# A hybrid decoder layer: TensorE's work of the retention block in program order, products of ones while it waits for loads, and first factors summed by TensorE alone

## The chip, the cores and the metric

The kernel runs on one core of one Trainium2 chip. The core has a tensor engine (TensorE; PE in the profile, with its weight loads listed apart as PEld), a vector engine (VectorE, DVE), a scalar engine (ScalarE, ACT), a general engine (GpSimd, POOL) and a queue that issues transfers (SyncE, SP); ACT can issue transfers too. Each engine works through its own instructions in order and waits for others by semaphores. The metric is the device time of one execution in microseconds (us), smaller is better.

## The reference, cut to what matters

One decoder layer on x of 1024 positions by 1024 channels, in float32. The change lies in its first third: the modulation of x by c, and the retention heads.

```python
mod = silu(c) @ w_ada + b_ada                 # six vectors of 1024
sh1, sc1, g1, sh2, sc2, g2 = split(mod)
h = x * (1.0 + sc1) + sh1
proj = h @ w_in                               # q, k, v, forget gates; rq, rk, rv, rg
fox = forgetting_attention(fq, fk, fv, log_sigmoid(ff + b_f))     # 8 heads of 64
ret = retention(rq, rk, rv, rg)                                   # 4 heads of 128
...
def retention(q, k, v, g):                    # q and k are rotated by position first
    ...
    def step(R, xs):                          # over 8 chunks of 128 positions
        s = einsum('bhnd,bhmd->bhnm', qi, ki) * inner
        o = einsum('bhnm,bhmv->bhnv', s, vi) + einsum('bhnd,bhdv->bhnv', qi, R) * xi
        R = R * g_chunk + einsum('bhmd,bhmv->bhdv', ki * zeta, vi)
        return R, o
    ...
    return silu(g) * normalised(o)
...
x = layer_norm(ALPHA * x + g1 * (concat(fox, ret) @ w_out))
h = x * (1.0 + sc2) + sh2                     # then the MLP with a convolution, and a second norm
```

## The kernel before, in words

Every large product is made from three: the operands are split into a high part (fp32r) and the low rest, and TensorE adds high x high, high x low and low x high in PSUM (`three`). A wide product is 128 x 128 weights against 512 columns.

**First stage.** The contraction over the 1024 channels of h is cut into eight slices j of 128. For slice j the SP queue loads the weights of the modulation (`ada`, two tiles of 4 x 256), a slice of the first retention head's weights (`wrr`) and a slice of x transposed (`xt`), three slices ahead (`h_load`). The shift and the scale of the slice, called first factors here, are `m = sum over k of ada_k * cs_k`: DVE adds up most of the eight terms into `acc` (`h_acc`), and `h_mod` lets PE multiply the rest (`DIRECT`: two terms for the first three slices, one otherwise) and `acc` by one column each; these products have one column and write a few columns of the PSUM tile `m1`. ACT adds the bias (`mod`), makes `hhi` (the high part of the modulated x) and the modulated `xt`, and DVE makes `hlo = xt - hhi`. Then PE adds the slice to seven PSUM tiles (`fa`, `fb`: the chunks of 128 positions of head 0) by 21 wide products: seven with hhi and the weights' high part, seven with their low part (among which the next slice's `h_mod` is placed), seven with hlo.

**Retention.** What remains of the projection of the four heads goes chunk by chunk (`ret_proj`, 24 wide products into a PSUM tile `rp`, in two halves of 12). `ret_evac` copies a chunk to SBUF and rotates it (POOL and DVE). The recurrence of a chunk takes three groups of small products, in three half-steps that follow one another: `ret_a` transposes q and k (`pq`, copied to `qkT` by ACT), `ret_b` makes the scores and the chunk's part of the state (`pS`; DVE weights the scores to `sT` and updates `R`), `ret_c` makes the output (`po`). `emit(t)` writes the groups that belong to half-step t between two halves of the projection. When a head's chunks are done, DVE and POOL normalise and gate it (`ret_norm`, `ret_gate`) and PE transposes it (`ret_out`, `py`). Beside that, DVE adds up the other four modulation vectors from `ada2` (`mod_piece`, `macc`), which PE closes with one-column products `mc` or two row products `mr` (`mod_end`). Last comes the projection of v and of the forget gates (`v_proj`, `vp`).

**What sets the order.** All of this stands in one block that a planner orders: it simulates the engines in time and picks for each engine what it believes to be ready, so the order of the code counts only where the code says so. `queued(key, ...)` says so: each call stands behind the last one of the same key on its engine. Before the change it is used for the loads, the ACT and DVE work and the first factors of the first stage; the wide products and all of the retention are left to the planner. The rest of the kernel (attention, output projection, MLP) follows after about 300 us.

The line numbers in the profile are those of the kernel below. What goes through `queued` is listed under L230 (the first call of a key under L232), since that is where the instruction is made; `three` is L207 to L209.

Of the kernel before, what the change touches and what calls it, by code (L numbers as in the profile page):

```python
# [15 lines left out]
P = 128  # L16
# [15 lines left out]
def kernel(  # L32
# [69 lines left out]
    cs = cp.tile([P, ND], F32, tag="cs", name="cs")  # L102
    nc.sync.dma_start(cs, cT)
# [6 lines left out]
    nc.vector.tensor_tensor(out=cs, in0=cs, in1=cse, op=ALU.mult)  # L110
    for i in (0, 2):
        nc.vector.tensor_scalar(
            out=bcol[:, i, :], in0=bcol[:, i, :], scalar1=1.0, scalar2=None, op0=ALU.add
        )
    mod2 = cp.tile([P, 2, ND], F32, tag="mod2", name="mod2")
# [29 lines left out]
    def bcast_rows(src, n):  # L145
        return bass.AP(tensor=src.tensor, offset=src.offset, ap=[[0, P], [1, n]])


    gates = dp.tile([2, D], F32, tag="gates", name="gates")
# [16 lines left out]
    def mod_end(m, acc):  # L166
        if m < 2:
            pt = bank(f"mc{m}")
            for j in range(ND):
                nc.tensor.matmul(  # L170
                    pt[:, j:j + 1], acc[:, j * P:(j + 1) * P], ones[:, 0:1],
                    start=True, stop=True,
                )
            nc.vector.tensor_tensor(
                out=mod2[:, m, :], in0=pt[:, :ND], in1=bcol[:, 2 + m, :], op=ALU.add
            )
            return
        row = slot("R", [1, D], F32, f"grow{m}")
        nc.sync.dma_start(row, b_rows[m - 2:m - 1, :])
        for n in range(2):  # L180
            sl = slice(n * 512, (n + 1) * 512)
            pt = bank(f"mr{m}_{n}")
            nc.tensor.matmul(pt[0:1, :], ones[:, 0:1], acc[:, sl], start=True, stop=True)
# [8 lines left out]
    def ret_w(h, j, raw):  # L192
        tag = "X" if h % 2 == 0 else "VM"
        w = slot(tag, [P, 2, 512], F32R, f"wr{h}_{j}")
        nc.scalar.copy(w[:, 0, :], raw)
# [9 lines left out]

    def three(pt, ahi, alo, whi, wlo, start, stop):
        nc.tensor.matmul(pt, ahi, whi, start=start, stop=False)  # L207
        nc.tensor.matmul(pt, ahi, wlo, start=False, stop=False)  # L208
        nc.tensor.matmul(pt, alo, whi, start=False, stop=stop)  # L209

# [9 lines left out]

    DIRECT = {0: 2, 1: 2, 2: 2}

    hs = {}
    order = {}

    def queued(key, fn, *args, **kw):

        if key in order:
            with tc.issue_after(order[key].ins):
                order[key] = fn(*args, **kw)  # L230
        else:
            order[key] = fn(*args, **kw)  # L232

    def ret_consts():
# [11 lines left out]
        return tr, dec, rc, bfb, lnc, cw  # L246

    def h_load(j):
        if j >= ND:
            return  # L250
        a = [slot("VM", [P, 4, 256], F32, f"ada1_{j}_{k}") for k in range(2)]
        for k in range(2):
            queued("SP", nc.sync.dma_start, a[k], ada1[j, :, 4 * k:4 * k + 4, :])
        raw = slot("R", [P, 512], F32, f"wrr0_{j}")
        queued("SP", nc.sync.dma_start, raw, w_ret[0, :, j, :])
        xt = slot("VM" if j % 2 else "S", [P, S], F32, f"xt{j}")
        queued("SP", nc.sync.dma_start, xt, xT[j * P:(j + 1) * P, :])
        hs[j] = (a, raw, xt)
# [29 lines left out]
    def h_mod(j):  # L288
        a, _, xt, acc = hs[j]
        pt = m1[:, 2 * j:2 * j + 2]  # L290
        for i in range(2):
            sl = slice(i * P, (i + 1) * P)
            n = DIRECT.get(j, 1)
            for k in range(ND - n, ND):
                queued(
                    "PE", nc.tensor.matmul, pt[:, i:i + 1], a[k // 4][:, k % 4, sl],
                    cs[:, k:k + 1], start=(k == ND - n), stop=False,
                )
            queued("PE", nc.tensor.matmul, pt[:, i:i + 1], acc[:, sl], ones[:, 0:1],
                   start=(n == 0), stop=True)  # L300
        for i in range(2):
# [5 lines left out]
        sc, sh = mod1[:, j, 0:1], mod1[:, j, 1:2]  # L307
        queued("ACT", nc.scalar.activation, hi, xt, AF.Identity, scale=sc, bias=sh)
        queued("ACT", nc.scalar.activation, xt, xt, AF.Identity, scale=sc, bias=sh)
        hhi.append(hi)  # L310

    def h_lo(j):
# [3 lines left out]
        hlo.append(lo)  # L316


    for j in range(3):
        h_load(j)  # L320
    h_cast(0)
    h_acc(0)
    h_low(0)
    h_mod(0)
    w1 = []
    for j in range(ND):
        h_load(j + 3)
        if j + 1 < ND:
            h_cast(j + 1)
            h_acc(j + 1)  # L330
        h_lo(j)
        if j + 1 < ND:
            h_low(j + 1)
        if j + 3 == ND:
            tr, dec, rc, bfb, lnc, cw = ret_consts()
        if j + 1 == ND:
            with tc.issue_after(order["ACT"].ins):
                for q in range(0, ND, 2):
                    ret_load(1, q, w1)
            queued("SP", nc.sync.dma_start, cw, conv)  # L340
        hi, lo = hhi[j], hlo[j]
        for c in range(7):
            nc.tensor.matmul(first[c], hi[:, c * P:(c + 1) * P], w0[j][:, 0, :],
                             start=(j == 0), stop=False)
        for c in range(7):
            if c == 3 and j + 1 < ND:
                h_mod(j + 1)
            order["PE"] = nc.tensor.matmul(first[c], hi[:, c * P:(c + 1) * P], w0[j][:, 1, :],
                                           start=False, stop=False)
        for c in range(7):  # L350
            nc.tensor.matmul(first[c], lo[:, c * P:(c + 1) * P], w0[j][:, 0, :],
                             start=False, stop=(j == ND - 1))

# [3 lines left out]
    def ret_proj(h, c, ws, part, pt):  # L357
        if part == 0:
            pt = bank2(f"rp{h}_{c}")[:, :512]
        for j in range(4 * part, 4 * part + 4):  # L360
            three(pt, hhi[j][:, c * P:(c + 1) * P], hlo[j][:, c * P:(c + 1) * P],
                  ws[j][:, 0, :], ws[j][:, 1, :], j == 0, j == ND - 1)
        return pt
# [21 lines left out]
    def ret_a(h, c, st):  # L385
        row = st["st"][c // 2][:, c % 2, :]
        pq = bank(f"pq{h}_{c}")
        nc.tensor.transpose(pq[:, 0:128], row[:, 0:P], ident)
        nc.tensor.transpose(pq[:, 128:256], row[:, P:2 * P], ident)
        qkT = tmp([P, 256], F32, f"qkT{h}_{c}")  # L390
# [10 lines left out]
    def ret_b(h, c, st):  # L401
        row = st["st"][c // 2][:, c % 2, :]
        qkT, v = st["qkT", c], row[:, 2 * P:3 * P]
        pS = bank(f"pS{h}_{c}")
        nc.tensor.matmul(pS[:, 0:128], qkT[:, 128:256], qkT[:, 0:128], start=True, stop=True)
        if c < NT - 1:
            nc.tensor.matmul(pS[:, 128:256], st["kz"], v, start=True, stop=True)
        sT = sp.tile([P, P], F32, tag="sT", bufs=2, name=f"sT{h}_{c}")
# [13 lines left out]
    def ret_c(h, c, st):  # L422
        row = st["st"][c // 2][:, c % 2, :]
        q, v = row[:, 0:P], row[:, 2 * P:3 * P]
        po = bank(f"po{h}_{c}")
        nc.tensor.matmul(po[:, 0:128], st["sT"], v, start=True, stop=(c == 0))
        if c > 0:
            nc.tensor.matmul(
                po[:, 0:128], st["qkT", c][:, 0:128], st["R"][c - 1], start=False, stop=True
            )  # L430
# [40 lines left out]
    def ret_out(h, half, st):  # L471
        pt = bank(f"py{h}_{half}")
        for i in range(4):
            c = half * 4 + i
            nc.tensor.transpose(
                pt[:, i * P:(i + 1) * P], st["st"][c // 2][:, c % 2, 0:P], ident
# [123 lines left out]
    def v_proj(c, n):  # L600
        n0, n1 = (0, 256) if n == 0 else (256, 520)
        pt = bank2(f"vp{c}_{n}") if c % 2 else bank(f"vp{c}_{n}")
        for j in range(ND):
            three(pt[:, :n1 - n0], hhi[j][:, c * P:(c + 1) * P],
                  hlo[j][:, c * P:(c + 1) * P],
                  wv[j][:, 0, n0:n1], wv[j][:, 1, n0:n1], j == 0, j == ND - 1)
        if n == 1:
# [47 lines left out]
    def cum_forget(Lp):  # L655
        pc = bank("pcum")
        nc.tensor.matmul(pc[:, :64], tri, L.rearrange("p c h -> p (c h)"),
                         start=True, stop=False)
        nc.tensor.matmul(pc[:, :64], ones, Lp.rearrange("p c h -> p (c h)"),
                         start=False, stop=True)  # L660
# [5 lines left out]
    def cum_store(cum):  # L666
        pc = bank("pcumT")
        nc.tensor.transpose(pc[:64, :P], cum.rearrange("p c h -> p (c h)"), ident)
        cumT = tmp([64, P], F32, "cumT")
# [898 lines left out]
```

## Time and profile before

| | |
|---|---|
| median of 3 runs | 1253.63 us (1252.91 to 1255.43) |
| the profiled execution | 1255.27 us, span from first to last instruction 1253.5 us |
| TensorE busy | 1220.3 us, 97% of the span |
| VectorE, ScalarE, GpSimd busy | 929.4, 630.9 and 247.9 us |
| mean granted clock of TensorE | 0.994 |
| first wide product of the first stage | at 12.72 us |
| first product of the rest of the projection (`rp`) | at 64.33 us |
| projection of v and of the gates (`vp`) | from 243.9 us to about 300 us |

The times in the profile's rows are us from the start of the span. A row in order of time gives the start, the duration, engine and line, the operation with the tiles it writes and reads, how many such instructions are merged, and in brackets how long the engine sat idle before and what released it. Matmuls overlap one another, so that the pace is read from one start to the next. A float32 product of TensorE is listed as two instructions, an fp32r product and a transpose as one. The granted clock is given by the throttle's records; in the first 17 us of the span these read 1.00 while equal products take twice as long as later, so there the speed is read from the starts.

### The profile page before, as it was taken

The page shows a single profiled execution, that of the slowest core. Times are in us where ns is not written, and L with a number is a line of the kernel's source. Part 1 is how long each engine was busy: PE and PEld are TensorE (multiplying, and loading weights), DVE is VectorE, ACT ScalarE, POOL GpSimd, SP SyncE. Part 2 cuts the span into 40 slices and gives each one's busy share as a digit, 9 for nine tenths or more (in the row PEclk, how much of TensorE's full clock was granted, in tenths as well). Part 3 has the DMA queues.
Part 4 walks back from the last instruction along what each step waited for, and adds up shares of the span by engine and source line. Part 5 has one row for each costly group of instructions (what it writes and reads, how often), then busy time and mean ns, then how long its engine had stood idle before and what let it go on. Part 6 is the DMA issues. An engine that isn't in the chain of part 4 may idle for free.

```text
span 1253.5 us, 17244 instructions
## 1 busy us (share of the span) xinstructions
PE 1220.3 (97%) x6077; PEld 1017.6 (81%) x6077; DVE 929.4 (74%) x1774; ACT 630.9 (50%) x1144; POOL 247.9 (20%) x293
## 2 busy tenths in 40 slices
PE   6999999999999999899999999999999999999997
PEld 5788888898888887788788888888888878888886
DVE  6774685884787777846888778778778785876686
ACT  3633233333676667476865444545445464634352
POOL 0034252500333333500003221321100101000021
PEclk9999999999999999999999999999999999999999
DMA  9623143443134234323238877976544588965751
GB/s 353 214 89 135 59 134 124 151 137 120 52 118 143 91 104 151 135 76 109 85 114 208 190 187 197 215 184 165 148 137 127 143 245 265 346 218 185 269 185 67
DMA packets 86046, 199.79 MB, mean 159 GB/s; under 512 B 9860, under 2 KB 16196, under 8 KB 85960
## 3 DMA queue, kind: packets, MB, share of 16 engines
q1 hardware_dynamic: 73288, 175.62, 40.6%
q0 software_dynamic: 12672, 23.07, 11.6%
q8 instruction: 48, 0.79, 0.2%
q14 instruction: 38, 0.31, 0.1%
HBM read 165.06 MB, written 68.20 MB: 186 GB/s over the span
## 4 chain that ended last, share of the span: by engine, by line
PE 85%; DVE 7%; ACT 3%; DMA 3%; issue 1%; SPq 0%; POOL 0%; DVEq 0%; ACTq 0%; POOLq 0%
PE dX L1307 10%; PE dZ L1307 7%; PE uX L1123 6%; PE uX L1124 6%; PE uX L1125 6%; PE uY L1125 4%; PE uY L1124 4%; PE uY L1123 4%; PE rp L208 3%; PE rp L209 3%; PE rp L207 3%; PE pv L793 3%; DMA xt<-in_xT_dram 2%; PE qk L709 2%; PE qk L710 2%; PE qk L711 2%
## 5 line engine op out<-in xcount | busy, mean ns | idle before, releaser
L1296 DVE TENSOR_TENSOR dl<-dr,dh 128x1024 fp32r<-128x1024 f32 x66 | 80.1, 1238 | 36.6 <-ACT dh L1284 35.7
L1284 ACT CAST dh<-dr 128x1024 fp32r<-128x1024 f32 x66 | 67.9, 1050 | 75.0 <-DMA dr<-in_w_down_dram 35.4
L755 POOL TENSOR_TENSOR S<-S,dn 128x128 f32<-128x128 f32 (+3 forms) x64 | 74.0, 1161 | 150.6 <-DVE dn L754 97.7
L970 POOL DMA_DIRECT2D sd<-gd x22 | 18.1, 823 | 394.3 <-DMA sd<-y 230.3
L207 PE MATMUL rp<-wr,hhi 128*128 128x512 f32 x200 | 79.0, 395 | 1.3 <-ACT rst L367 1.3
L208 PE MATMUL rp<-wr,hhi 128*128 128x512 f32 x200 | 79.1, 396 | 0.5 <-POOL wr L197 0.5
L209 PE MATMUL rp<-wr,hlo 128*128 128x512 f32 x200 | 78.8, 394 | 0.0
L1307 PE MATMUL dX<-dl,dh 128*128 128x512 f32 x176 | 68.5, 389 | 0.0
L1307 PE MATMUL dX<-dh 128*128 128x512 f32 x176 | 68.5, 389 | 0.0
L1307 PE MATMUL dX<-dh,dl 128*128 128x512 f32 x176 | 68.5, 389 | 0.0
L1138 ACT COPY u<-uX 128x512 f32<-128x512 f32 x44 | 25.8, 586 | 72.7 <-PE uX L1125 72.7
L751 ACT ACTIVATE S<-S,mn 128x128 f32<-128x128 f32 (+3 forms) x64 | 49.9, 779 | 15.1 <-DVE mn L746 13.9
L709 PE MATMUL qk<-hhi,wqh 128*128 128x512 f32 x128 | 54.6, 426 | 0.0
L784 DVE TENSOR_TENSOR pt<-pt,pt 128x512 fp32r<-128x512 f32 (+2 forms) x96 | 50.8, 550 | 4.3 <-ACT pt L783 3.1
L746 DVE CUSTOM_DVE_ANT_0 S<-ps,nb 128x128 f32<-128x128 f32 (+3 forms) x64 | 48.0, 750 | 8.0 <-PE ps L744 5.6
L793 PE MATMUL pv<-pt,V 128*128 128x256 f32 x320 | 49.8, 293 | 2.4 <-DVE pt L784 1.2
L208 PE MATMUL op<-wol,mxs 128*128 128x512 f32 x128 | 50.4, 394 | 1.7 <-DVE wol L893 1.5
L711 PE MATMUL qk<-hhi,wql 128*128 128x512 f32 x128 | 51.6, 403 | 0.0
L207 PE MATMUL op<-woh,mxs 128*128 128x512 f32 x128 | 50.7, 398 | 0.9 <-DVE mn L746 0.9
L1307 PE MATMUL dZ<-dh 128*128 128x512 f32 x132 | 51.6, 391 | 0.0
L1307 PE MATMUL dZ<-dl,dh 128*128 128x512 f32 x132 | 51.4, 389 | 0.0
L1307 PE MATMUL dZ<-dh,dl 128*128 128x512 f32 x132 | 51.4, 389 | 0.0
(1057 smaller groups left out, 3830.6 us busy)
## 6 DMA issues: line engine op xcount, KB each, us to landing
ada<-in_ada_dram SPq DMA_DIRECT2D x48, 512.0 KB, 4.0
td<-in_w_down_dram SPq DMA_DIRECT2D x44, 256.0 KB, 5.5
wa<-in_w_up_dram SPq DMA_DIRECT2D x22, 512.0 KB, 5.0
wb<-in_w_up_dram SPq DMA_DIRECT2D x22, 512.0 KB, 4.0
gd<-y SPq DMA_DIRECT2D x22, 512.0 KB, 2.7
sd<-y SPq DMA_DIRECT2D x44, 256.0 KB, 3.6
dr<-sd SPq DMA_DIRECT2D x44, 256.0 KB, 4.4
dr<-td SPq DMA_DIRECT2D x44, 256.0 KB, 3.9
```

Of the source, the lines that this page charges most:

```text
L207: nc.tensor.matmul(pt, ahi, whi, start=start, stop=False)
L208: nc.tensor.matmul(pt, ahi, wlo, start=False, stop=False)
L209: nc.tensor.matmul(pt, alo, whi, start=False, stop=stop)
L709: nc.tensor.matmul(pt, whi[:, j, :], hhi[j][:, sl], start=(j == 0), stop=False)
L711: nc.tensor.matmul(pt, wlo[:, j, :], hhi[j][:, sl], start=False, stop=(j == ND - 1))
L755: nc.gpsimd.tensor_tensor(out=Ssb[:, :span], in0=Ssb[:, :span], in1=den.to_broadcast([P, span]), op=ALU.mult,)
L793: nc.tensor.matmul(pv[:, :256], V2[h][:, kb, :], pts[kb // 4][u][:, kb % 4, :], start=(kb == 0 and u == 0), stop=(kb == nkb - 1 and u == 1),)
L1123: nc.tensor.matmul(pt, whi, bh, start=start, stop=False, skip_group_check=True)
L1124: nc.tensor.matmul(pt, whi, bl, start=False, stop=False, skip_group_check=True)
L1125: nc.tensor.matmul(pt, wlo, bh, start=False, stop=stop, skip_group_check=True)
L1296: nc.vector.tensor_tensor(out=lo, in0=raw, in1=f(hi), op=ALU.subtract)
L1307: nc.tensor.matmul(pt, w_[:, 0, q], m_[:, 1, :], start=start and n_ == 0, stop=stop and n_ == 2, skip_group_check=True)
```

## The change

Six edits, all in the block of the first stage and the retention:

1. TensorE's work of the block goes through `queued("PE", ...)`, in the order in which the code is written: the wide products of the first stage, `ret_proj`, `v_proj`, the groups of small products, the transposes, `mc` and `mr`. In the first stage the code now writes the next slice's first factors as one piece ahead of the last ten wide products (ahead of the last six for slice 0). The first half-step of the recurrence is one later (`2 * NT - 1`).
2. `keep_on`: eleven products of `ones` with `ones` at the start and seven after the first factors of slice 0, into columns of `m1` that nothing reads.
3. The first factors of slice 0 are summed by TensorE alone (`DIRECT[0] = ND`): 16 one-column products, no `acc`.
4. `cs` and `bcol` are loaded through ACT's queue; the addition of 1 to `bcol` stands later on DVE. `xt` of slice 0 is loaded and turned to `hhi` in two halves.
5. From slice 3 on, the first of the terms of `acc` is made by ACT.
6. The casts of head 1's weights on ACT are set by `queued`: two of the eight ahead of slice 7's `mod`, the others behind its `xt`; the low parts follow on DVE.

```diff
     cs = cp.tile([P, ND], F32, tag="cs", name="cs")
-    nc.sync.dma_start(cs, cT)
+    nc.scalar.dma_start(cs, cT)
     bcol = cp.tile([P, 4, ND], F32, tag="bcol", name="bcol")
-    nc.sync.dma_start(bcol, b_cols)
+    nc.scalar.dma_start(bcol, b_cols)
...
@@ ret_w @@
+        if h == 1:
+            queued("ACT", nc.scalar.copy, w[:, 0, :], raw)
+            return w, raw
         nc.scalar.copy(w[:, 0, :], raw)
-        eng = nc.vector if h == 1 else nc.gpsimd
-        eng.tensor_tensor(out=w[:, 1, :], in0=raw, in1=f(w[:, 0, :]), op=ALU.subtract)
+        nc.gpsimd.tensor_tensor(out=w[:, 1, :], in0=raw, in1=f(w[:, 0, :]), op=ALU.subtract)
...
+    def in_turn(*args, **kw):
+        queued("PE", nc.tensor.matmul, *args, **kw)
+
+    def turn(*args):
+        queued("PE", nc.tensor.transpose, *args)
...
-    DIRECT = {0: 2, 1: 2, 2: 2}
+    DIRECT = {0: ND, 1: 2, 2: 2}
...
+    def h_cuts(j):
+        return [slice(0, 512), slice(512, S)] if j == 0 else [slice(0, S)]
...
@@ h_acc @@
-        acc = tmp([P, 256], F32, f"acc1_{j}")
-        for k in range(ND - DIRECT.get(j, 1)):
+        n = ND - DIRECT.get(j, 1)
+        acc = tmp([P, 256], F32, f"acc1_{j}") if n else None
+        for k in range(n):
             src = a[k // 4][:, k % 4, :]
-            if k == 0:
+            if k == 0 and j > 2:
+                queued("ACT", nc.scalar.activation, acc, src, AF.Copy, scale=cs[:, 0:1])
+            elif k == 0:
...
+    def keep_on(n):
+
+        for _ in range(n):
+            in_turn(m1[:, 256:384], ones, ones, start=True, stop=True)
...
     for j in range(3):
         h_load(j)
+    keep_on(11)
+    for i in (0, 2):
+        queued("DVE", nc.vector.tensor_scalar,
+               out=bcol[:, i, :], in0=bcol[:, i, :], scalar1=1.0, scalar2=None, op0=ALU.add)
     h_cast(0)
     h_acc(0)
     h_low(0)
     h_mod(0)
+    keep_on(7)
...
+        if j + 2 == ND:
+            ret_load(1, 0, w1)
         h_lo(j)
...
         if j + 1 == ND:
-            with tc.issue_after(order["ACT"].ins):
-                for q in range(0, ND, 2):
-                    ret_load(1, q, w1)
+            for q in range(2, ND, 2):
+                ret_load(1, q, w1)
             queued("SP", nc.sync.dma_start, cw, conv)
+            for w, raw in w1:
+                queued("DVE", nc.vector.tensor_tensor, out=w[:, 1, :], in0=raw,
+                       in1=f(w[:, 0, :]), op=ALU.subtract)
+            w1 = [w for w, _ in w1]
         hi, lo = hhi[j], hlo[j]
-        for c in range(7):
-            nc.tensor.matmul(first[c], hi[:, c * P:(c + 1) * P], w0[j][:, 0, :],
-                             start=(j == 0), stop=False)
-        for c in range(7):
-            if c == 3 and j + 1 < ND:
+        seq = [(c, t) for t in range(3) for c in range(7)]
+        for n, (c, t) in enumerate(seq):
+            if n == (15 if j == 0 else 11) and j + 1 < ND:
                 h_mod(j + 1)
-            order["PE"] = nc.tensor.matmul(first[c], hi[:, c * P:(c + 1) * P], w0[j][:, 1, :],
-                                           start=False, stop=False)
-        for c in range(7):
-            nc.tensor.matmul(first[c], lo[:, c * P:(c + 1) * P], w0[j][:, 0, :],
-                             start=False, stop=(j == ND - 1))
+            in_turn(first[c], (hi, hi, lo)[t][:, c * P:(c + 1) * P],
+                    w0[j][:, (0, 1, 0)[t], :],
+                    start=(j == 0 and t == 0), stop=(j == ND - 1 and t == 2))
...
-        nc.tensor.transpose(pq[:, 0:128], row[:, 0:P], ident)
-        nc.tensor.transpose(pq[:, 128:256], row[:, P:2 * P], ident)
+        turn(pq[:, 0:128], row[:, 0:P], ident)
+        turn(pq[:, 128:256], row[:, P:2 * P], ident)
...
-        ta = max(2 * n + A0, 2 * NT - 2 + n)
+        ta = max(2 * n + A0, 2 * NT - 1 + n)
```

The same replacement by `in_turn` or `turn` stands at `three` in `ret_proj` and `v_proj`, at `pS`, `po`, `py`, `mc`, `mr` and the two `pcum` products.

How this stands on PE, at three places. In these rows `m` is the PSUM tile of the first factors, `fa` one of the seven tiles of the first stage, `wr` a slice of weights, and the numbers count buffers.

PE at its start, up to the first wide product, before:

```order
L232 MATMUL m_107<-cs,ada_0_1_110 128x1
L230 MATMUL m_107<-cs,ada_0_1_110 128x1
L230 MATMUL m_107<-ones,acc_0_135 128x1
L230 MATMUL m_107<-cs,ada_0_1_110 128x1 x2
L230 MATMUL m_107<-ones,acc_0_135 128x1
L343 MATMUL fa_102<-wr_0_133,hhi_151 128x512 x2
```

and now:

```order
L152 MATMUL m_105<-ones 128x128
L150 MATMUL m_105<-ones 128x128 x10
L150 MATMUL m_105<-cs,ada_0_0_107 128x1 x4
L150 MATMUL m_105<-cs,ada_0_1_108 128x1 x4
L150 MATMUL m_105<-cs,ada_0_0_107 128x1 x4
L150 MATMUL m_105<-cs,ada_0_1_108 128x1 x4
L150 MATMUL m_105<-ones 128x128 x7
L150 MATMUL fa_100<-wr_0_145,hhi_166 128x512 x2
```

Eleven products of ones, sixteen first factors and seven products of ones stand where six first factors stood, two of which wait for DVE's sum `acc`.

PE in the middle of slice 6, where the first factors of slice 7 stand, before:

```order
L348 MATMUL fa_103<-wr_6_411,hhi_451 128x512
L230 MATMUL m_107<-cs,ada_7_1_361 128x1
L348 MATMUL fa_103<-wr_6_411,hhi_451 128x512
L348 MATMUL fb_104<-wr_6_411,hhi_451 128x512
L348 MATMUL fb_105<-wr_6_411,hhi_451 128x512
L348 MATMUL fb_106<-wr_6_411,hhi_451 128x512
L230 MATMUL m_107<-ones,acc_7_467 128x1
L230 MATMUL m_107<-cs,ada_7_1_361 128x1
L230 MATMUL m_107<-ones,acc_7_467 128x1
L351 MATMUL fa_102<-wr_6_411,hlo_475 128x512 x2
```

and now:

```order
L150 MATMUL fa_101<-wr_6_434,hhi_475 128x512 x2
L150 MATMUL m_105<-cs,ada_7_1_384 128x1
L150 MATMUL m_105<-ones,acc_7_490 128x1
L150 MATMUL m_105<-cs,ada_7_1_384 128x1
L150 MATMUL m_105<-ones,acc_7_490 128x1
L150 MATMUL fb_102<-wr_6_434,hhi_475 128x512
L150 MATMUL fb_103<-wr_6_434,hhi_475 128x512
L150 MATMUL fb_104<-wr_6_434,hhi_475 128x512
L150 MATMUL fa_100<-wr_6_434,hlo_504 128x512 x2
```

The four first factors stood in two pieces, the last three ahead of the last seven wide products; now they stand in one, ahead of the last ten.

PE in head 1's recurrence, chunks 1 to 5, before (`po`, `pS`, `pq` are the three groups, `py` the transposes of the head that is done):

```order
L428 MATMUL po_2_1126<-R_1_1028,qkT_2_1033 128x128
L405 MATMUL pS_3_1133<-qkT_3_1094 128x128
L407 MATMUL pS_3_1133<-rst_1_675,kz_3_1096 128x128
L388 MATMUL pq_4_1163<-ident,rst_2_676 128x128
L389 MATMUL pq_4_1163<-ident,rst_2_676 128x128
L426 MATMUL po_3_1198<-rst_1_675,sT_3_1136 128x128
L428 MATMUL po_3_1198<-R_2_1089,qkT_3_1094 128x128
L405 MATMUL pS_4_1205<-qkT_4_1166 128x128
L407 MATMUL pS_4_1205<-rst_2_676,kz_4_1168 128x128
L388 MATMUL pq_5_1233<-ident,rst_2_676 128x128
L389 MATMUL pq_5_1233<-ident,rst_2_676 128x128
L475 MATMUL py_0_1244<-ident,rst_0_565 128x128 x2
```

and now, in the same head (the rows from `rp_6` on go on to twelve wide products):

```order
L150 MATMUL po_2_1168<-R_1_1070,qkT_2_1075 128x128
L150 MATMUL pS_3_1175<-qkT_3_1141 128x128
L150 MATMUL pS_3_1175<-rst_1_684,kz_3_1143 128x128
L150 MATMUL pq_4_1182<-ident,rst_2_685 128x128 x2
L150 MATMUL rp_6_1204<-wr_0_500,hhi_166 128x512 x2
L150 MATMUL rp_6_1204<-wr_0_500,hlo_194 128x512
L150 MATMUL rp_6_1204<-wr_1_502,hhi_220 128x512 x2
L150 MATMUL rp_6_1204<-wr_1_502,hlo_246 128x512
L150 MATMUL rp_6_1204<-wr_2_541,hhi_268 128x512 x2
```

Five groups of small products stood one behind another with no wide product between them; now twelve wide products stand between any two.

More of the change, by code (lines that the diff above doesn't have):

```diff
@@ L182, in mod_end @@
             pt = bank(f"mr{m}_{n}")
-            nc.tensor.matmul(pt[0:1, :], ones[:, 0:1], acc[:, sl], start=True, stop=True)
+            queued("PE", nc.tensor.matmul, pt[0:1, :], ones[:, 0:1], acc[:, sl],
+                   start=True, stop=True)
             nc.vector.tensor_tensor(
@@ L290, in h_mod @@
         pt = m1[:, 2 * j:2 * j + 2]
+        n = DIRECT.get(j, 1)
         for i in range(2):
             sl = slice(i * P, (i + 1) * P)
-            n = DIRECT.get(j, 1)
             for k in range(ND - n, ND):
[L295 to L300, printed above, removed]
+                in_turn(pt[:, i:i + 1], a[k // 4][:, k % 4, sl], cs[:, k:k + 1],
+                        start=(k == ND - n), stop=(k == ND - 1 and acc is None))
+            if acc is not None:
+                in_turn(pt[:, i:i + 1], acc[:, sl], ones[:, 0:1], start=(n == 0), stop=True)
         for i in range(2):
@@ L404, in ret_b @@
         pS = bank(f"pS{h}_{c}")
-        nc.tensor.matmul(pS[:, 0:128], qkT[:, 128:256], qkT[:, 0:128], start=True, stop=True)
+        in_turn(pS[:, 0:128], qkT[:, 128:256], qkT[:, 0:128], start=True, stop=True)
         if c < NT - 1:
-            nc.tensor.matmul(pS[:, 128:256], st["kz"], v, start=True, stop=True)
+            in_turn(pS[:, 128:256], st["kz"], v, start=True, stop=True)
         sT = sp.tile([P, P], F32, tag="sT", bufs=2, name=f"sT{h}_{c}")
@@ L667, in cum_store @@
         pc = bank("pcumT")
[L668 removed]
+        turn(pc[:64, :P], cum.rearrange("p c h -> p (c h)"), ident)
         cumT = tmp([64, P], F32, "cumT")
```

50 lines of the change are left out of this document (25 added, 25 removed).

## The prediction

> **What bounds the kernel now.** I read the page first, then who waited for whom on TensorE (PE), then all engines in order of time over the first 70 us, and last PE and VectorE (DVE) around the one long wait in the middle.
>
> ```profile
> PE 1220.3 (97%) x6077; PEld 1017.6 (81%) x6077; DVE 929.4 (74%) x1774; ACT 630.9 (50%) x1144; POOL 247.9 (20%) x293
> ...
> PE m L232 <- DMA ada<-in_ada_dram: 7.4, 1, 7.4
> PE po L426 <- DVE sT L409: 3.1, 3, 2.1
> ...
> PE rp L207 <- ACT rst L367: 1.3, 1, 1.3
> ```
>
> PE is the bound: 97% busy, and what a change can gain is PE's idle time and its slow time. The waits that this change can reach are 7.4 us for the first load, one of 2.1 us for a decay-weighted score tile sT, and 1.3 us for an eviction. The rows in order of time show more:
>
> ```profile
> 0.81 0.39 SPq L103 DMA_DIRECT2D cs<-in_cT_dram  x1
> ...
> 0.94 0.17 DVE L88 MEMSET ones<- 128x128 f32 x1
> ...
> 1.72 0.43 SPq L232 DMA_DIRECT2D ada<-in_ada_dram  x1
> ...
> 6.06 0.35 DVE L232 TENSOR_SCALAR acc<-ada,cs 128x256 f32<-128x256 f32 x1 [1.45 <-DMA ada<-in_ada_dram]
> ...
> 9.53 0.99 PE L230 MATMUL m<-cs,ada 128*128 128x1 f32 x4
> ...
> 10.38 0.57 PE L230 MATMUL m<-ones,acc 128*128 128x1 f32 x2
> ...
> 10.98 0.41 ACT L230 ACTIVATE mod<-m,bcol 128x1 f32<-128x1 f32 x2 [2.38 <-PE m L230]
> ...
> 11.27 0.35 DVE L230 TENSOR_SCALAR acc<-ada,cs 128x256 f32<-128x256 f32 x1 [1.65 <-DMA ada<-in_ada_dram]
> 11.43 1.24 ACT L230 ACTIVATE hhi<-xt,mod 128x1024 fp32r<-128x1024 f32 x1
> ...
> 12.72 2.07 PE L343 MATMUL fa<-wr,hhi 128*128 128x512 f32 x4 [1.78 <-ACT hhi L230]
> ...
> 14.15 1.22 DVE L230 TENSOR_TENSOR hlo<-xt,hhi 128x1024 fp32r<-128x1024 f32 x1
> ...
> 15.87 1.48 PE L348 MATMUL fa<-wr,hhi 128*128 128x512 f32 x3
> ...
> 18.11 0.86 PE L348 MATMUL fb<-wr,hhi 128*128 128x512 f32 x3
> ...
> 21.53 1.21 PE L343 MATMUL fa<-wr,hhi 128*128 128x512 f32 x4
> ```
>
> Nothing useful runs on PE before 12.72. The first seven wide products then take 15.87 - 12.72 = 3.15 us, 0.45 each, while three at 18.11 take 0.86 in place of 1.48 at 15.87: PE comes to full speed 4.4 to 5.4 us after steady work begins. Slice j = 1 of the first stage begins at 21.53.
>
> ```profile
> 51.91 1.19 PE L343 MATMUL fa<-wr,hhi 128*128 128x512 f32 x4
> ...
> 56.02 1.17 PE L351 MATMUL fa<-wr,hlo 128*128 128x512 f32 x4
> ...
> 57.94 1.19 PE L343 MATMUL fa<-wr,hhi 128*128 128x512 f32 x4
> ...
> 59.07 4.25 ACT L195 CAST wr<-wrr 128x512 fp32r<-128x512 f32 x8
> ...
> 59.66 1.07 PE L348 MATMUL fa<-wr,hhi 128*128 128x512 f32 x4
> ...
> 61.25 1.07 PE L351 MATMUL fa<-wr,hlo 128*128 128x512 f32 x4
> ...
> 63.23 1.05 ACT L367 COPY rst<-fa 128x512 f32<-128x512 f32 x2
> 64.33 0.50 PE L207 MATMUL rp<-wr,hhi 128*128 128x512 f32 x1 [1.33 <-ACT rst L367]
> ```
>
> A slice lasts 57.94 - 51.91 = 6.03 us. Seven products take 61.25 - 59.66 = 1.59, so 21 take 4.77 (0.227 each). The last first factor precedes 56.02 and the next slice waits for its hhi until 57.94: a chain of 1.92 us through ScalarE (ACT) over which only seven products (1.59) stand now. The last slice is followed by eight casts, two copies, and only then the first rp product at 64.33.
>
> ```profile
> 136.60 0.39 PE L428 MATMUL po<-R,qkT 128*128 128x128 f32 x2
> 136.82 0.39 PE L405 MATMUL pS<-qkT 128*128 128x128 f32 x2
> ...
> 137.38 0.27 PE L389 MATMUL pq<-ident,rst 128*128 128x128 f32 x1
> 139.71 0.49 PE L426 MATMUL po<-rst,sT 128*128 128x128 f32 x2 [2.06 <-DVE sT L409]
> ...
> 140.26 0.39 PE L405 MATMUL pS<-qkT 128*128 128x128 f32 x2
> ...
> 142.54 0.64 PE L428 MATMUL po<-R,qkT 128*128 128x128 f32 x2
> 142.97 0.63 PE L405 MATMUL pS<-qkT 128*128 128x128 f32 x2
> ...
> 144.03 0.27 PE L389 MATMUL pq<-ident,rst 128*128 128x128 f32 x1
> ...
> 148.94 1.84 PE L170 MATMUL mc<-ones,macc 128*128 128x1 f32 x16
> ...
> 140.00:150.00 10.00, 10.00 (x56) 9.08 (x55) 7.79 (x25) 3.01 (x10) 3.01 (x7) 0.83 0.25 79
> ...
> 137.49 1.97 DVE L465 TENSOR_SCALAR rst<-rst,mv,gr 128x128 f32<-128x128 f32 x5
> ...
> 139.38 0.28 DVE L409 TENSOR_TENSOR sT<-pS,dec 128x128 f32<-128x128 f32 x1
> ```
>
> Here small products stand without wide ones between them; sT comes behind five of DVE's gate products, PE idles 2.06 us, and then a 128x128 product takes 142.97 - 142.54 = 0.43 in place of 136.82 - 136.60 = 0.22: the granted clock averages 0.83 over these 10 us. A one-column product is two instructions: 1.84 / 8 = 0.23 us at full speed, and (10.38 - 9.53) / 2 = 0.43 at half.
>
> **The change, part by part.**
>
> Loads. cs and bcol leave SP's queue, so the first load is issued at 0.81 in place of 1.72. Its queue then stays full, so all loads of the stage, in the same order as before, should come 0.9 us earlier: the first half of slice 0's factors at 6.06 - 0.91 = 5.15, of slice 1's at 10.36. The two small loads now stand ahead of ACT's table load; cs is still ready before 5.15. I take 0.9; the bounds are 0 and 0.9.
>
> Products of ones. They need only ones (ready 1.11). Eleven at 0.43 run from 1.2 to 5.9, over time in which PE idled; if the rise takes 4.4 to 5.4 us again, full speed comes at 5.6 to 6.6. They write a corner of a tile that nobody reads.
>
> First factors by PE alone. Sixteen products replace six on PE and six instructions on DVE. From 5.9, about one slow, the rest at 0.23: end near 9.7 (bounds 9.6 and, all slow, 12.8), against 10.95 now. The second seven ones take 1.5 us, to 11.25; ACT meanwhile makes two mods (0.45) and half of hhi (0.62), so the xt cut in two lets PE start on the half. Start of wide products: 11.25, at full speed.
>
> Slice 0. Fourteen products end at 11.25 + 3.18 = 14.4. The fifteenth needs hlo, which on DVE stands behind slice 1's sum: 10.36 + (14.15 - 11.27) + 1.22 = 14.5, so the load bounds this, not the clock. Then one product 0.23, six first factors 1.38, and the chain of 1.92: slice 1 starts at 18.0 against 21.53, 3.5 earlier.
>
> Slices 1 to 6. The first factors now stand together ahead of the last ten products: 10 x 0.227 = 2.27 covers 1.92, so PE never waits. Slice 1 costs 4.77 + 1.38, each of the next five 4.77 + 4 x 0.23 = 5.69 against 6.03: slice 7 at 18.0 + 6.15 + 28.45 = 52.6 against 57.94, 5.3 earlier. DVE loses one 0.35 us instruction a slice to ACT (from slice 3 on); both stay under 5.69. Its cover is thin on ACT: two casts more before slice 7.
>
> End of the stage. Two of eight casts are done a slice earlier. Six at 0.52 start 1.13 us after the slice (59.07 - 57.94), then the two copies (1.10): first rp at 52.6 + 1.13 + 3.12 + 1.10 = 57.95. **Gain up to here: 64.33 - 57.95 = 6.4.** What is late next is the same copies, 0.6 behind PE.
>
> Retention in program order. Twelve wide products (2.73 us) stand between any two groups of small ones, so the bunch at 134 to 144 is gone: sT has 2.73 us of cover, the gap of 2.06 goes, and the slow time too. From 140.26 to 144.14 six products (0.22 each at full speed) and eight transposes (half that) take 3.9 us in place of 2.2: 1.7 lost. **Gain 3.8** (bounds 0, if DVE is late there all the same, and 4.8, if the other 1.0 of PE's 3.1 for sT goes as well).
>
> The Trainium skill, "TensorE: Matmul & The Clock Gate", section "Why this matters for your kernels", allows idle gaps up to about 3 us before the clock falls. By it a gap of 2.06 would cost itself alone, and the sum would be 1.7 us smaller. The trace differs: 0.83 follows the gap.
>
> The price of the fixed order: PE stands where the scheduler let it go on.
>
> ```profile
> 78.12 0.28 DVE L409 TENSOR_TENSOR sT<-pS,dec 128x128 f32<-128x128 f32 x1
> ...
> 64.33:100.00 35.67, 35.67 (x180) 30.26 (x181) 25.54 (x70) 8.81 (x23) 12.73 (x24) 1.00 0.28 89
> ```
>
> DVE reaches the first sT 78.12 - 64.33 = 13.8 us after the first rp, behind the rotation of eight chunks. The new order asks for it after 24 + 12 + 12 wide products (10.9) and 0.9 of small ones: 11.8 us. With 0.3 for sT itself PE would wait 2.3; I take 1.6, since part of the 13.8 is DVE's own waiting for others. Elsewhere DVE has 28% spare (25.54 of 35.67 busy); for the rest, and for the column products mc, which now follow their DVE sum at once where the scheduler had set 21 wide products ahead of them, I allow 0.7. **Loss 2.3** (bounds 0 and, 0.5 at each of the twelve groups more, 8).
>
> **Sum.** 6.4 + 3.8 - 2.3 = 7.9. The profiled execution took 1255.27 (span 1253.5, 1.77 around it), so 1247.4 by it; the median of the runs lies 1.64 below that execution: 1245.7. After 300 us the order on the engines is as before, and PE stays the bound, so the gain should reach the end whole.
>
> **The rivals.**
>
> 1. The clock stays at half speed through the first factors, since one-column products keep little of PE busy; the products at 9.53 and 10.38 did not stop 12.72 from being slow. Then they end at 12.8, the second ones (0.43 each) at 15.8, slice 1 starts at 15.8 + 3.4 + 1.4 + 1.9 = 22.5: 4.5 worse, 1250.2. The Trainium skill (same page, "Part 1") has a free-running window of about 3.4 us, by which full speed would come between 4.6 and 8.0. No row here shows what such products count for.
> 2. PE is never held by DVE: no 2.3, and the other 1.0 of waits for sT goes as well: 1242.4. Against it stand the 13.8 us at 78.12.
> 3. The bunch goes but DVE's gate products hold PE all the same: no 3.8, 1249.5. The rows at 137.49 speak for it, the 2.73 us of cover against.
> 4. The other side: DVE is the bound of the fixed order. Its work for a group must now fit into 3.8 us (12 wide products and 1.1 of small ones), where the old order had some 20 wide ones, 5.6 us. At 72% busy before, that may ask for all of it, and PE waits for sT at every group. From about 1.0 us at each of the first twelve groups and one fall of the clock on, the loss passes 6.4 + 3.8 + 2.5 = 12.7 and the kernel is slower by over 0.2%: 1257. Against it: much of DVE's work there, the rotation of the eight chunks, comes before the groups.
>
> **Chances.** Forecast (1244 to 1248.5) 0.62; rival 1 0.12; rival 2 0.12; rival 3 0.08; rival 4 0.06, of it 0.04 slower. 0.2% is 2.5 us, about what a measurement tells from none: faster means under 1251.1. Rival 1 counts two thirds as faster. Faster 0.88, same 0.08, slower 0.04. The range from rival 2 to a little past rival 1, 1242 to 1250.5, leaves out under 2 in 10.
>
> **What would show it.** Wide products from about 11.3 at 0.227; slice 1 at 18, a slice every 5.7, first rp near 58; a wait of po for sT of 1 to 2 us near 70; no clock below 1.00 near 130; span near 1245.6. Wrong if one-column products take 0.43 past 8 us, if slices stay at 6.0, or if po <- sT adds up to more than 5 us.

## The result, and the profile after

The changed kernel takes 1264.65 us (median of 4 runs, 1264.54 to 1264.95) against 1253.85 us of the kernel before beside it (4 runs): a ratio of 1.0085, 95% interval 1.0068 to 1.0103. It is slower by 10.8 us; 1245.7 was forecast, 7.9 us faster. The profiled execution took 1264.75 us, its span is 1263.0 in place of 1253.5.

In the profile after, everything that goes through `queued` stands under L150. What PE waited for, from the view of waits:

```profile
PE m L150 <- DVE acc L150: 6.8, 4, 2.1
PE po L150 <- DVE sT L434: 3.9, 2, 2.1
...
PE pq L150 <- DVE rst L406: 1.1, 1, 1.1
```

The first row is four waits of a first factor's product for the DVE sum. Before, such a wait came once, 0.7 us in slice 0, and none of the rivals had more of them. The place where the time went is found with three marks in the order of time: the start of slice 1, the first rp product and the last vp product.

| mark | before | forecast | after |
|---|---|---|---|
| slice 1 starts | 21.53 | 18.0 | 21.62 |
| first rp | 64.33 | 57.95 | 75.22 |
| from there to the last vp | 235.4 | 233.9 | 234.9 |
| from there to the end | 953.8 | the same | 952.9 |

So the whole loss of 9.5 us, and more, lies between slice 1 and the first rp. One turn of the loop there, all engines in order of time (rows of slices 2 to 4):

```profile
30.40 0.28 PE L150 MATMUL m<-cs,ada 128*128 128x1 f32 x2
...
32.73 0.38 PE L150 MATMUL m<-ones,acc 128*128 128x1 f32 x2 [2.05 <-DVE acc L150]
...
33.78 1.63 PE L150 MATMUL fb<-wr,hhi 128*128 128x512 f32 x3
...
33.96 0.41 ACT L150 ACTIVATE mod<-m,bcol 128x1 f32<-128x1 f32 x2 [4.40 <-PE m L150]
34.40 1.24 ACT L150 ACTIVATE hhi<-xt,mod 128x1024 fp32r<-128x1024 f32 x1
...
35.68 1.24 ACT L150 ACTIVATE xt<-xt,mod 128x1024 f32<-128x1024 f32 x1
...
36.82 0.60 ACT L150 CAST wr<-wrr 128x512 fp32r<-128x512 f32 x1
...
37.33 0.51 ACT L150 ACTIVATE acc<-ada,cs 128x256 f32<-128x256 f32 x1
...
37.87 3.09 DVE L150 SCALAR_TENSOR_TENSOR acc<-ada,cs,acc 128x256 f32<-128x256 f32 x6 [3.46 <-ACT acc L150]
...
41.65 0.36 PE L150 MATMUL m<-ones,acc 128*128 128x1 f32 x2
...
42.49 0.41 ACT L150 ACTIVATE mod<-m,bcol 128x1 f32<-128x1 f32 x2 [4.66 <-PE m L150]
```

Read it as one chain. The first term of a slice's sum, which the change gives to ACT from j = 3 on, stands in ACT's queue behind hhi and xt of the slice before and a cast. These wait for that slice's mod at 33.96, so DVE cannot begin the sum before 37.87, and ends it 3.0 us later; the product that closes it makes the next mod. ACT is then idle for 4.66 us, and DVE was idle for 3.46 us: neither is full, yet from mod to mod it takes 8.5 us in this turn (0.7 of it since PE, slow, asks late for the sum). From the mod at 33.96 to that of slice 7 at 66.41 are four turns of 8.1 us, where PE has 5.69 us of work for a slice.

The waits cost twice. After the one at 32.73 three wide products take 1.63 in place of 0.85 us: PE is at half clock. From the table of stretches of 1 us of the same profile (PE busy with count, granted clock, DMA share, GB/s):

```profile
9.00:10.00 1.00, 1.00 (x8) 0.57 0.97 322
...
15.00:16.00 1.00, 1.00 (x4) 0.52 1.03 408
33.00:34.00 1.00, 1.00 (x7) 0.52 1.05 404
...
39.00:40.00 1.00, 1.00 (x4) 0.57 0.05 20
50.00:51.00 1.00, 1.00 (x6) 0.55 0.00 0
...
53.00:54.00 1.00, 1.00 (x5) 0.74 0.12 18
```

A mean of 0.52 in the stretch from 33 says that the clock fell to 0.5 at 33.04; the 0.57 from 39, that it rose at 39.86. Half speed lasted from 33.04 to 39.86, from 50.10 to 53.52, and once more for 3.4 us from 67.2 on: 13.7 us at half speed are 6.8 us lost. With 6.8 us of waits that is 13.6. From the start of slice 1 to the first rp it took 42.8 us before and takes 53.6 now; without the 13.6 it would be 40.0.

### The profile page after: what moved, and what is told of

It is laid out like the page before. It is cut to its first block, busy times and chain, and to the rows that moved or that the text cites. A ratio compares the mean times of both kernels' runs of the same rounds, so it can differ in the third digit from the quotient of the medians.

```text
span 1263.0 us, 17347 instructions
## 1 busy us (share of the span) xinstructions
PE 1230.6 (97%) x6133; PEld 1028.3 (81%) x6133; DVE 925.0 (73%) x1763; ACT 634.2 (50%) x1150; POOL 249.4 (20%) x293
## 4 chain that ended last, share of the span: by engine, by line
PE 80%; DVE 11%; ACT 3%; DMA 3%; issue 3%; SPq 0%; DVEq 0%; POOL 0%; ACTq 0%; POOLq 0%
PE rp L150 9%; PE dX L1332 7%; PE uX L1149 6%; PE uX L1148 6%; PE uX L1150 6%; PE dZ L1332 5%; PE uY L1150 4%; PE uY L1149 4%; PE uY L1148 4%; PE vp L150 4%; PE pv L818 3%; PE qk L734 2%; PE qk L735 2%; PE qk L736 2%; PE pt L802 2%
## 5 line engine op out<-in xcount | busy, mean ns | idle before, releaser
L150 PE MATMUL rp<-wr,hhi 128*128 128x512 f32 x400 | 128.1, 401 | 0.0
L150 PEld LDWEIGHTS rp<-wr,hhi 128*128 128x128 f32 x400 | 71.5, 189 | 13.1 <-ACT rst L392 0.5
L150 PE MATMUL rp<-wr,hlo 128*128 128x512 f32 x200 | 78.5, 392 | 0.0
```

## The experiments

The medians below are compared with the kernel before that ran beside them (1253.81 to 1254.30). The runs of most of these kernels scatter over 3 to 6 us; the last section names a likely cause. e1 to e4, e5 to e8 and e9 to e11 ran in three groups, between which the kernel before moved by up to 0.5 us; a difference between kernels of two groups carries that too.

| kernel | median us (runs) | ratio to before, 95% |
|---|---|---|
| e1_dve_first_term | 1253.61 (10) | 0.9994, 0.9985 to 1.0003 |
| e2_mod_late | 1278.59 (4) | 1.0192, 1.0175 to 1.0209 |
| e3_no_ones | 1254.16 (10) | 1.0000, 0.9990 to 1.0009 |
| e4_mid_planner | 1252.13 (10) | 0.9985, 0.9976 to 0.9994 |
| e5_sum_start | 1249.90 (7) | 0.9962, 0.9951 to 0.9974 |
| e6_ones_among | 1254.99 (10) | 1.0006, 0.9997 to 1.0016 |
| e7_old_start | 1249.14 (4) | 0.9959, 0.9944 to 0.9974 |
| e8_later_scores | 1253.03 (9) | 0.9982, 0.9971 to 0.9994 |
| e9_act_term_early | 1253.77 (10) | 0.9998, 0.9989 to 1.0008 |
| e10_first_ones | 1250.79 (8) | 0.9973, 0.9963 to 0.9983 |
| e11_old_start_fixed | 1251.14 (10) | 0.9980, 0.9971 to 0.9989 |

**The chain.** Three kernels ask whether it is ACT's queue that closes it.

```diff
-            if k == 0 and j > 2:
-                queued("ACT", nc.scalar.activation, acc, src, AF.Copy, scale=cs[:, 0:1])
-            elif k == 0:
+            if k == 0:
```

> The changed kernel, with the first term of every slice's sum on DVE again (slices 3 to 7 had it on ACT). Theory A: on ACT that term stands behind hhi, xt and the cast of the slice before, which all wait for that slice's mod, so mod to mod is one chain of 8 us (0.45 + 1.28 + 1.14 + 0.5 + 0.54 on ACT, 3.0 for six DVE instructions, 0.9 of products and some 0.2 between them); the four waits of m for acc (6.8 us) and the slow clock after three of them (6.8 us) follow from it. Taken away: no such wait, slices at 5.7 from 27.9 on, first rp near 62 in place of 75.2, time near 1251.4 (1250 to 1253). Theory B: the place itself is too early, since the fixed order asks for a sum after 11 of 21 products whoever makes its first term: the waits stay at 1 to 2 us a slice, time over 1260.

This one step is worth 11.0 us. The waits of m for acc are gone and slices come every 5.71 us (PE, in order of time):

```profile
27.98 1.07 PE L150 MATMUL fa<-wr,hhi 128*128 128x512 f32 x4
...
33.69 1.07 PE L150 MATMUL fa<-wr,hhi 128*128 128x512 f32 x4
...
39.40 1.07 PE L150 MATMUL fa<-wr,hhi 128*128 128x512 f32 x4
```

The first rp is at 61.50. Theory B is out. The median is 2.2 us above what A named; the profile spends that after the first rp (237.2 us from there to the last vp in place of 234.9, see the last section). So without the chain the rest of the change is no gain that can be told: a ratio of 0.9994, with 1 inside its interval.

```diff
-            if n == (15 if j == 0 else 11) and j + 1 < ND:
+            if n == (15 if j == 0 else 18) and j + 1 < ND:
```

> The changed kernel (first term on ACT), with the next slice's first factors issued after 18 of 21 products in place of 11. Theory A (one chain of 8 us from mod to mod): where on PE they stand doesn't shorten the chain; PE's wait moves and is split, part before the sum's product and part before the next hhi; mod to mod stays at 7.6 to 8.1, time 1262 to 1267. Theory B (the place is too early): the waits for acc vanish, 1.2 us is left before each hhi, slices at 6.9, time near 1257.

Both numbers missed: it is 14 us slower than the changed kernel. All engines, one turn:

```profile
48.05 0.42 ACT L150 ACTIVATE mod<-m,bcol 128x1 f32<-128x1 f32 x2 [6.35 <-PE m L150]
...
51.43 0.51 ACT L150 ACTIVATE acc<-ada,cs 128x256 f32<-128x256 f32 x1
...
51.96 3.09 DVE L150 SCALAR_TENSOR_TENSOR acc<-ada,cs,acc 128x256 f32<-128x256 f32 x6 [5.40 <-ACT acc L150]
...
54.97 1.22 DVE L150 TENSOR_TENSOR hlo<-xt,hhi 128x1024 fp32r<-128x1024 f32 x1
...
56.24 1.20 PE L150 MATMUL fa<-wr,hlo 128*128 128x512 f32 x4 [2.99 <-DVE hlo L150]
...
58.62 0.41 ACT L150 ACTIVATE mod<-m,bcol 128x1 f32<-128x1 f32 x2 [6.69 <-PE m L150]
```

A chain it is, but a longer one: in DVE's queue hlo stands behind the sum, and on PE the first factors now stand behind four products with hlo. So 1.22 of DVE and 0.9 of PE join the loop: 58.62 - 48.05 = 10.6 us. A later place does not shorten the wait; it ties in what it is moved behind.

```diff
             if n == (15 if j == 0 else 11) and j + 1 < ND:
+                h_first(j + 2)
                 h_mod(j + 1)
```

(`h_first(j + 2)` issues the ACT term of slice j + 2's sum.)

> The changed kernel whole, but ACT makes the first term of a slice's sum ahead of the mod of the slice before (one place earlier in ACT's queue) in place of behind its cast. Theory A (the place in the queue closes the chain from mod to mod): the waits of m for acc go as in e1_dve_first_term, slices at 5.7, first rp near 61.5, time 1252 to 1255. Theory F (a term on ACT costs by itself, as a slower instruction or as a hand-over between two engines in the sum): waits stay, time over 1258.

As A said. The term is still on ACT; in ACT's rows it now stands before the mod that it used to wait for, and mods follow one another in 5.71 us:

```profile
31.42 0.41 ACT L150 ACTIVATE mod<-m,bcol 128x1 f32<-128x1 f32 x2 [1.82 <-PE m L150]
...
34.80 0.51 ACT L150 ACTIVATE acc<-ada,cs 128x256 f32<-128x256 f32 x1
37.13 0.41 ACT L150 ACTIVATE mod<-m,bcol 128x1 f32<-128x1 f32 x2 [1.83 <-PE m L150]
```

With e1 this shows the cause: not a term on ACT, but its place behind the mod of the slice before and what follows that mod.

**The start.** e3 is e1 without the ones.

```diff
-    keep_on(11)
...
-    keep_on(7)
```

> As e1_dve_first_term, without the eleven and the seven products of ones (nothing that is read is left out). Theory C: the ones bring the clock up by 6 us, but one-column products don't hold it, so it falls at 9.1 and the second ones and the first wide products run at half speed. Without ones the 16 first factors take 0.43 each from 6.2 to 13, wide products start near 14.2 as now and stay slow until about 19.4 in place of 16.0: slice 1 near 23 in place of 21.6, time 1 to 2 us over e1. Theory D: the ones only stand in the way: wide products start near 12 in place of 14.0, time 1 to 2 us under e1.

In the profile C holds: slice 1 at 23.54 in place of 21.69 in e1. By the medians the ones are worth 0.55 us, less than the runs scatter. The next three stand on e4's planner order in retention (below).

```diff
-    DIRECT = {0: ND, 1: 2, 2: 2}
+    DIRECT = {0: 2, 1: 2, 2: 2}
...
-    keep_on(11)
+    keep_on(26)
```

> As e4_mid_planner, with slice 0's first factors summed on DVE again (six terms of eight), so that PE has 6 one-column products there in place of 16, and 26 products of ones in place of 11 ahead of them, so that PE has work until the sum is there. Theory C (one-column products don't hold the clock, products of ones do): no fall of the clock before the wide products, which start near 11.5 to 12.5 at 0.227 each in place of 15.3 at 0.45; slice 1 near 18.5 to 19.5 in place of 23.4 (21.7 in e1), time 2.5 to 4.5 us under e4. Theory D (the clock decides nothing here, since slice 0 waits for DVE's and ACT's work anyway): slice 1 not before 21.5, time within 1 us of e4.

2.2 us under e4, but not by the way that C named: slice 1 starts at 21.32, not 19 (PE, in order of time).

```profile
10.09 0.38 PE L150 MATMUL m<-ones,acc 128*128 128x1 f32 x2 [0.99 <-DVE acc L150]
...
11.64 3.24 PE L150 MATMUL m<-ones 128*128 128x128 f32 x14 [0.50 <-ACT mod L150]
14.64 1.17 PE L150 MATMUL fa<-wr,hhi 128*128 128x512 f32 x4
```

The clock falls at 11.2 for one spell of 3.4 us all the same, and the seven second ones, at half speed, hold PE until 14.64. They also wait 0.50 for ACT, which still reads mod's source from the tile that the ones write.

```diff
                         start=(k == ND - n), stop=(k == ND - 1 and acc is None))
+                if j == 0 and k % 2 == 1:
+                    in_turn(first[6][:, 0:128], ones, ones, start=True, stop=True)
```

> As e4_mid_planner, with a product of ones after every second of slice 0's 16 first factors (eight in all, into a corner that the first wide product overwrites). Theory C, if a third of PE's time in products of ones is enough for the clock: first factors at full speed, over by 12, wide products from 13.5 at 0.227, slice 1 near 20.5, time 1 to 2.5 us under e4. If a third is too little, or if the clock falls for another reason: the clock is half from 8 or 9 on, the eight cost 0.43 each, slice 1 near 25, time 1 to 2.5 us over e4.

The second case, a little beyond its range: 2.9 us over e4. In the profile (the slowest of the ten executions) products are slow from the start to about 20, by their starts, so neither the eleven first ones in this execution nor a third of the time in ones was enough.

```diff
-    keep_on(26)
...
-    keep_on(7)
```

> As e5_sum_start without any products of ones: the start is that of the kernel before, with the loads of cs and bcol still on ACT's queue. Theory C: wide products start at 12.7 to 13.7 and are slow for 3 to 5 us as before; slice 1 near 21.5 to 22.5, time within 1.2 us of e4 and 2.5 to 4 us over e5. Theory D: the same time as e5 within 1 us.

The lowest median of all, 5.2 us under the kernel before, with no ones at all; the intervals of this kernel and e5 overlap almost whole. Neither theory holds as it stands: the time is within 1 us of e5, as D says, but not for D's reason. Here wide products start earlier and slow, in e5 later and fast, and both reach 17.9 for the fifteenth; the two effects happen to cancel:

```profile
13.27 2.08 PE L150 MATMUL fa<-wr,hhi 128*128 128x512 f32 x4 [1.35 <-ACT hhi L150]
...
17.90 0.39 PE L150 MATMUL fa<-wr,hlo 128*128 128x512 f32 x1
...
21.30 1.19 PE L150 MATMUL fa<-wr,hhi 128*128 128x512 f32 x4 [0.27 <-ACT hhi L150]
```

```diff
     h_mod(0)
-    keep_on(7)
```

> As e5_sum_start without the seven second products of ones (the 26 first ones stay). If the second ones are what holds the first wide products back (3.2 us at half speed in e5, where hhi was there 1.3 us after mod): wide products from 12.8 to 13.3, slice 1 near 20 in place of 21.3, time 0.5 to 1.5 us under e7_old_start. If the first ones bring nothing, because a fall of the clock at the one-column products takes back what they gave: within 0.7 us of e7.

Outside both: 1.65 us over e7. Wide products start at 12.28, but the clock falls at 11.1, they stay slow until 17.9, and slice 1 starts at 21.57, 0.3 later than in e7. The two profiles differ by more, 2.5 us, in retention, where this execution had a fall of the clock near 137 and e7's had none, though both had the same wait of 2.06 us for sT just before. In e5 and e7 the first rp starts at 61.14 and 61.11: what the ones give there they also cost. What the first ones alone are worth stays open.

**The fixed order in retention.** e4 is e1, and e7 is e11, with PE's retention work left to the planner.

```diff
-        in_turn(pS[:, 0:128], qkT[:, 128:256], qkT[:, 0:128], start=True, stop=True)
+        nc.tensor.matmul(pS[:, 0:128], qkT[:, 128:256], qkT[:, 0:128], start=True, stop=True)
...
```

> As e1_dve_first_term, with PE's work after the first stage (retention and v_proj) left to the planner, as in the kernel before; the first stage stays in program order. Theory E: the fixed order there is worth next to nothing, since DVE's gate products and the late first sT hold PE for 5.0 us in place of 3.1 us of waits and 1.7 us of slow clock: time within 1.5 us of e1, first rp to last vp near 235. The forecast's reading: the fixed order is worth 1.5 us or more: e4 over e1 by 1.5 to 4.

> As e7_old_start, with the fixed program order in retention and v_proj again (the changed kernel's). Theory E: the fixed order costs 1.5 to 4 us against the planner's there, in waits of po for sT and pq for rst (near 5.5 in e1) and falls of the clock behind them: 1250.5 to 1253. The forecast's reading (the fixed order gains): 1246 to 1249.

The planner's order (of the retention and of v_proj) is 1.5 us faster in the one pair and 2.0 in the other. The intervals overlap, widely in the first pair and barely in the second; both point the same way, and against the forecast. What holds PE in the fixed order, in the profile of the changed kernel (all engines):

```profile
129.84 1.00 DVE L490 TENSOR_SCALAR rst<-rst,mv,gr 128x128 f32<-128x128 f32 x3
...
130.97 1.97 DVE L490 TENSOR_SCALAR rst<-rst,mv,gr 128x128 f32<-128x128 f32 x5
...
132.86 0.28 DVE L434 TENSOR_TENSOR sT<-pS,dec 128x128 f32<-128x128 f32 x1
...
133.28 0.46 PE L150 MATMUL po<-rst,sT 128*128 128x128 f32 x2 [1.80 <-DVE sT L434]
```

sT stands behind the eight gate products of the head before, as at 137.49 in the old kernel. With the 2.12 us of the first po (89.47) and 1.12 behind the next rotation these are 5.0 us; before they were 3.1 us and 1.7 of slow clock.

```diff
-        ta = max(2 * n + A0, 2 * NT - 1 + n)
+        ta = max(2 * n + A0, 2 * NT + n)
```

> As e1_dve_first_term (fixed order in retention), with the first groups of small products one step of 12 wide products later (16 in place of 15 in the table's formula). Theory E: the first wait of po for sT (2.7 us near 76 in e1) and the fall of the clock behind it go, since DVE gets 2.7 us more; the waits behind the gate products near 118 to 125 stay (1.8 and 1.1 in e1); time 2 to 4 us under e1 in its profile, 1.5 to 3.5 by the medians. If the wait moves along with the group, since DVE is the bound there: time within 1 us of e1.

The first wait is gone, as E said, and the one behind the gate products is longer, 3.65 us at 121.75, where eight gates took 4.75 us; the clock falls behind it. The profile is 3.7 us under that of e1, but it is the fastest of nine executions, and the median is 0.6 under: no gain that can be told.

## Why the prediction was wrong, step by step

By the profiled executions the forecast missed by 17.4 us (1264.75 against 1247.4): 3.6 up to slice 1, 13.6 from there to slice 7, nothing from slice 7 to the first rp, 1.0 in retention, and 0.9 back after it. The other 1.5 is the step from the profiled execution to the median: 1.64 was taken off, and it was 0.10.

- **Loads.** Half right. Slice 1's sum starts at 10.47 (10.36 forecast). But cs, on ACT's queue beside the large loads, is first read at 5.28 in place of 2.4 us, and PE's first factors start at 6.19. "cs is still ready before 5.15" was a guess without a row.
- **Products of ones.** They ran from 1.16 to 6.04 as said, and the first products behind them were fast. What failed is "from 5.9, about one slow, the rest at 0.23": the clock fell at 9.14 in the midst of the one-column products. They ended at 10.52 (9.7), the second ones took 3.0 us in place of 1.5, and wide products began at 14.02 (11.25), slow until 15.96. This is rival 1 in kind: slice 1 at 21.62, for which it had 22.5 and the forecast 18.0. It cost the forecast 3.6 us.
- **Slices 1 to 6, the step that failed.** "DVE loses one 0.35 us instruction a slice to ACT (from slice 3 on); both stay under 5.69." Both do (in a turn ACT is busy for 4.0 us and DVE for 5.0); that is a sum of busy times, and says nothing of a loop. Most links stood in the forecast's rows: the mod, hhi and cast on ACT, the sum on DVE. They were not added up from one mod to the next. By the rows after, mod, hhi, xt, cast and first term on ACT, the sum on DVE and the products that close it are 0.45 + 1.28 + 1.14 + 0.5 + 0.54 + 3.0 + 0.9 = 7.8, with hand-overs the 8.1 us measured, against the 5.69 of the forecast. Slice 7 starts at 69.86, forecast 52.6. e1 and e9 take the chain apart and give 5.71 a slice, as the forecast's sum has it without the chain.
- **End of the stage.** From slice 7's start to the first rp 5.36 us, forecast 5.35: right by luck. The forecast had the first rp wait for ACT's casts and copies. In the profile it waits for nothing: PE works through, at half speed for the first 0.7 us. In e1, without the slow time, the same stretch is 61.50 - 56.54 = 4.96.
- **Retention.** The bunch of small products is gone, as said; "2.73 us of cover" did not hold sT clear of eight gate products. So the waits and slow time of 4.8 us went and 5.0 us of waits came (2.3 had been allowed), as rival 3 had it: 0.5 us gained by the two profiles (235.4 to 234.9), and a loss of 1.5 to 2.0 by the medians against the planner's order in the same surroundings.
- **The side.** The slower case had 0.04. Rival 4 had DVE as the bound of retention; it came from ACT's place in the first stage.
- **The clock after a gap.** The trace was said to differ from the rule of the Trainium skill ("TensorE: Matmul & The Clock Gate", section "Why this matters for your kernels", no idle gaps above about 3 us). It did so again: three gaps of 2.05 to 2.11 us, at 32.73, 49.55 and 65.54, were followed by half speed. Two others, 2.12 at 89.47 and 1.80 at 133.28, were not.

## What to carry to other kernels

When an operation moves to another engine, ask not only whether that engine has time for it, but what it stands behind in that engine's queue, and follow the loop from one turn's result to the next: here no engine was full, and the loop still set the pace. In a fixed order on one engine, each wait holds all that is behind it; a later place only helps if it is not itself behind something that waits. Products that only keep the tensor engine busy are worth trying only with the kernel without them beside it: here no version with them was shown to be faster than the same one without.

## What the runs showed of the hardware

**The clock changes on a fixed grid.** The six changes shown above are at 9.14, 15.96, 33.04, 39.86, 50.10 and 53.52: 2, 7, 9, 12 and 13 times 3.41 us after the first ((53.52 - 9.14) / 13 = 3.414). This is the free-running window of about 3.4 us of the Trainium skill (same page, "Part 1"). What PE did in the windows that end at a fall, and in one that doesn't, by the grid worked out from those times:

```profile
5.73:9.14 3.41, 3.27 (x30) 1.00 1.07 379
29.63:33.04 3.41, 1.36 (x10) 1.00 1.03 407
46.69:50.10 3.41, 1.35 (x11) 1.00 0.01 2
...
63.75:67.16 3.41, 1.62 (x10) 1.00 0.00 0
87.64:91.05 3.41, 1.58 (x11) 1.00 0.34 131
```

The first four were followed by half clock, the last was not. The first is listed as 96% busy, almost all of it in one-column products: dense as they were, they did not hold the clock. Nor did they raise it in e3, where sixteen of them ran from 6.12 to 13.1 and the wide products from 14.46 on were slow. In the fourth, 0.7 us of the 1.62 is one-column, in the last nothing. So it is not the gap alone that decides. The likely reading, not shown by a run made for it, is that the work in the window does, and that the same gap falls into one window or into two, as the execution happens to lie on the grid. No run measured the threshold.

**That chance moves the time.** From the first rp to the last vp the fixed order took 237.2, 236.8 and 236.9 us in the three profiles where the clock fell behind the first po (e1, e3, e9), and 234.9, 234.6 and 235.2 in those where it did not (the changed kernel, e2, e11): about 2 us between them. Not all of that is the clock, since the first waits differ (1.62 to 2.67 us); e3 and e9 with 2.44 and a fall and e11 with 2.37 and none give 1.6 to 1.7, which is half of one spell of 3.41 us. It is a likely source of the scatter of most kernels here; the other runs left no trace to show it.
